# A two-layer decoder trunk on Trainium2: all 22 FFN tiles by block products, ten of them begun in the first token half

## The chip, the cores and the metric

The kernel runs on one core of one Trainium2 chip. The metric is the device time of one execution in microseconds (us): the median of several runs. The engines are named as the profile names them: PE (TensorE matmul), PEld (its weight loads), DVE (VectorE), ACT (ScalarE), POOL (GpSimd) and SP (SyncE, which issues the DMAs here).

## What is computed

Two layers, each a token mixer and a feed-forward network (FFN), on 1024 tokens of width 1024 in float32. Layer 0 mixes by gated linear attention, layer 1 by a gated delta rule. The FFN, 2816 wide, is the same in both:

```
def swiglu(h, w_gate_up, w_down):
    gate, up = jnp.split(h @ w_gate_up, 2, axis=-1)
    return (jax.nn.silu(gate) * up) @ w_down
...
        h = h + swiglu(rms_norm(h, ffn_norm_w[i]), ffn_w_gate_up[i], ffn_w_down[i])
```

## The kernel before

**Split numbers.** Every float32 operand is held as a sum hi + lo of two rounded parts. `operand` (L1114) makes them for 128x512 weights: hi by a cast on ACT (L1118), lo = src - hi on POOL (L1119). A product over k blocks of 128 rows is three matmuls per block (hi·hi, lo·hi, hi·lo, all at L201). A product over four blocks is so 12 matmuls into one 128x512 PSUM bank; over eight blocks it is 24.

**The two token halves.** The FFN works on 512 tokens at a time. The first half's normed input, called x or `head` (b11 its first four blocks, b21 the other four), is ready while the mixer still works on the second half. The mixer's last step is its output projection (`out`, 48 matmuls, w by o), and DVE adds its results into h (L316). Then comes the norm of the second half: sums of squares on ACT (L299) and DVE (L301), their total ns (L304), a reciprocal root in some ten small DVE operations, and from h and that the normed xn (L1160), which PE transposes (L1164).

**Two kinds of tiles.** A tile is 128 of the 2816 columns of gate and of up. Of the 22 tiles of a layer, 19 are computed by seven block products instead of eight: `inputsums` (L1135) makes the sums t1, t2, t3, t4 of the two halves' blocks on DVE, splits them (L1150, L1153), and `gateups` (L1198) makes the sums s1 to s4 of the four weight blocks a11, a12 (gate), a21, a22 (up) on DVE (L1208 to L1215). The seven products of 12 matmuls are a11·b11, s1·t1, s2·t2, a12·b21, s3·t3, s4·b22 and a22·t4, 84 matmuls a tile; they are added in three PSUM banks, which ACT copies out between the products (L1221 to L1230).

The other three tiles (HEAD = 3) are plain. `headparts` (L1068) computes gate and up for the first half, 24 matmuls each; after the first four blocks ACT copies what the bank holds (L1083) and SP stores it in DRAM as `part` (L1085). The end of `inputsums` (L1182 to L1196) makes the second half's gate and up from `part` (loaded at L1191) and products with t1 and b22 (`guweights`, L1121, loads the raw weights).

**Order.** In layer 0 `ffnhead` (L1064) emits the plain tiles' first halves behind the mixer. In layer 1 the order of PE is set by hand: `dense` in `gdn` is a stream of matmuls that fills the gaps of the delta rule's sequential chain, and its last two items are `headparts` and the last unit's output projection `out(UN - 1)`, which needs that unit's `post` (L1026: o scaled at L1036, transposed, gated by `gateout` at L344 to L346). Everywhere else a scheduler orders each engine's stream. The raw weights of a tile are four DMAs of 256 KB (L1130) into two buffers; the split operands have five (`wops`). `downs` is the product with w_down that follows.

## Time and profile before

| | |
|---|---|
| median of 3 runs | 3298.59 us (3297.29 to 3308.17) |
| the profiled execution | 3307.1 us, of which its span 3305.3 us |
| PE busy | 2980.4 us, 90% of the span, 14547 matmuls |
| DVE busy | 2105.8 us, 64% |
| POOL busy | 1527.4 us, 46% |
| ACT busy | 1401.0 us, 42% |
| mean granted TensorE clock | 0.956 of 2.4 GHz |

A row of a timeline gives the start, the duration, the engine, the line, what is written from what, and in brackets how long the engine sat idle before it and who released it. Busy PE is not PE at its peak: matmuls overlap, so that one is recorded as 0.39 us long and the next begins about 0.23 us after it. Durations and places in time below are those of the profiled execution.

### The profile page before, as it was taken

The page shows a single profiled execution, that of the slowest core. Times are in us where ns is not written, and L with a number is a line of the kernel's source. Part 1 is how long each engine was busy: PE and PEld are TensorE (multiplying, and loading weights), DVE is VectorE, ACT ScalarE, POOL GpSimd, SP SyncE. Part 2 cuts the span into 40 slices and gives each one's busy share as a digit, 9 for nine tenths or more (in the row PEclk, how much of TensorE's full clock was granted, in tenths as well). Part 3 has the DMA queues.
Part 4 walks back from the last instruction along what each step waited for, and adds up shares of the span by engine and source line. Part 5 has one row for each costly group of instructions (what it writes and reads, how often), then busy time and mean ns, then how long its engine had stood idle before and what let it go on. Part 6 is the DMA issues. An engine that isn't in the chain of part 4 may idle for free. (4 is left out here: it accounts for less than half of the span.)

```text
span 3305.3 us, 40855 instructions
## 1 busy us (share of the span) xinstructions
PE 2980.4 (90%) x14547; PEld 2452.3 (74%) x14547; DVE 2105.8 (64%) x4212; ACT 1401.0 (42%) x2525; POOL 1527.4 (46%) x1037
## 2 busy tenths in 40 slices
PE   6989989899998998879989897889899889999898
PEld 5877777678886777667777776777777668887776
DVE  6465665633324886778778868787788542232988
ACT  4345444434333334434445453444444434333333
POOL 4344443455555873513333333233333345554885
PEclk9999999899999999879999998999999999999999
DMA  3221222322222311312222222222232232222431
GB/s 123 77 58 58 64 64 71 104 93 77 83 83 100 133 67 41 83 31 69 70 72 69 59 59 64 64 65 67 63 77 63 84 112 78 89 83 77 143 105 58
DMA packets 364923, 256.39 MB, mean 78 GB/s; under 512 B 67848, under 2 KB 309967, under 8 KB 364719
## 3 DMA queue, kind: packets, MB, share of 16 engines
q1 hardware_dynamic: 364654, 253.77, 25.9%
q8 instruction: 114, 1.87, 0.2%
q14 instruction: 91, 0.74, 0.1%
q0 software_dynamic: 64, 0.02, 0.0%
HBM read 219.12 MB, written 34.60 MB: 77 GB/s over the span
## 5 line engine op out<-in xcount | busy, mean ns | idle before, releaser
L169 POOL TENSOR_TENSOR wlo<-raw,whi 128x1024 fp32r<-128x1024 f32 x204 | 493.3, 2420 | 772.8 <-ACT whi L168 724.5
L201 PE MATMUL pd<-xhi,whi 128*128 128x512 f32 x1072 | 450.6, 421 | 1.0 <-ACT part L1083 0.7
L201 PE MATMUL pd<-xhi,wlo 128*128 128x512 f32 x1072 | 429.6, 401 | 2.6 <-POOL wlo L169 2.6
L201 PE MATMUL pd<-xlo,whi 128*128 128x512 f32 x1072 | 427.4, 399 | 0.0
L168 ACT CAST whi<-raw 128x1024 fp32r<-128x1024 f32 x204 | 213.9, 1049 | 258.1 <-PE pd L201 133.4
L1119 POOL TENSOR_TENSOR olo<-s,ohi 128x512 fp32r<-128x512 f32 x152 | 196.0, 1291 | 206.7 <-ACT ohi L1118 206.7
L1119 POOL TENSOR_TENSOR olo<-raw,ohi 128x512 fp32r<-128x512 f32 x138 | 190.6, 1383 | 202.2 <-ACT ohi L1118 177.9
L201 PEld LDWEIGHTS pd<-xhi,wlo 128*128 128x128 f32 x1072 | 206.2, 192 | 50.9 <-POOL wlo L169 4.7
L201 PEld LDWEIGHTS pd<-xhi,whi 128*128 128x128 f32 x1072 | 207.0, 193 | 38.9 <-ACT part L1083 1.6
L201 PEld LDWEIGHTS pd<-xlo,whi 128*128 128x128 f32 x1072 | 207.3, 193 | 37.5
L1118 ACT CAST ohi<-s 128x512 fp32r<-128x512 f32 x152 | 94.3, 622 | 231.6 <-PE pd L201 175.0
L201 PE MATMUL pd<-whi,ohi 128*128 128x512 f32 x384 | 166.8, 435 | 12.3 <-ACT q L690 8.9
L886 DVE TENSOR_TENSOR xix<-xix,tmpx 128x60 f32<-128x60 f32 (+24 forms) x496 | 168.5, 340 | 13.1
L884 DVE TENSOR_TENSOR tmpx<-nbx,xix 128x60 f32<-128x60 f32 (+24 forms) x496 | 159.5, 322 | 26.3 <-DMA nbx<-d 13.5
L1118 ACT CAST ohi<-raw 128x512 fp32r<-128x512 f32 x138 | 85.1, 620 | 197.4 <-POOL olo L1119 174.3
L316 DVE TENSOR_TENSOR h<-h,pd 128x512 f32<-128x512 f32 x192 | 130.4, 682 | 55.0 <-PE pd L201 54.4
L201 PE MATMUL pd<-wlo,ohi 128*128 128x512 f32 x384 | 157.1, 409 | 2.0 <-POOL wlo L169 2.0
L201 PE MATMUL pd<-whi,olo 128*128 128x512 f32 x384 | 155.3, 404 | 0.0
L1275 POOL TENSOR_TENSOR blo<-t,bhi 128x1536 fp32r<-128x1536 f32 (+1 forms) x32 | 126.3, 3948 | 61.0 <-ACT bhi L1274 52.8
L1227 DVE TENSOR_TENSOR p<-p,pp 128x512 f32<-128x512 f32 x38 | 26.1, 688 | 196.3 <-DMA raw<-in_ffn_w_gate_up_dram 148.0
L201 PE MATMUL pd<-bhi,ahi 128*128 128x512 f32 x264 | 108.7, 412 | 36.4 <-DVE h L1285 20.1
L1275 POOL TENSOR_TENSOR blo<-rb,bhi 128x1536 fp32r<-128x1536 f32 (+1 forms) x24 | 97.8, 4074 | 42.6 <-ACT bhi L1274 42.6
(393 smaller groups left out, 8210.1 us busy)
## 6 DMA issues: line engine op xcount, KB each, us to landing
raw<-in_gdn_w_in_dram SPq DMA_DIRECT2D x96, 512.0 KB, 4.0
raw<-in_ffn_w_gate_up_dram SPq DMA_DIRECT2D x176, 256.0 KB, 3.3
raw<-in_gla_w_in_dram SPq DMA_DIRECT2D x48, 512.0 KB, 3.9
ra<-act SPq DMA_DIRECT2D x88, 256.0 KB, 5.3
rb<-in_ffn_w_down_dram SPq DMA_DIRECT2D x24, 768.0 KB, 6.5
raw<-in_gdn_w_out_dram SPq DMA_DIRECT2D x32, 512.0 KB, 3.9
act<-p SPq DMA_DIRECT2D x44, 256.0 KB, 2.0
act<-u SPq DMA_DIRECT2D x38, 256.0 KB, 2.0
```

The lines of the kernel that those rows point to most:

```text
L168: nc.scalar.copy(hi, raw)
L169: nc.gpsimd.tensor_tensor(out=lo, in0=raw, in1=hi.bitcast(F32), op=ALU.subtract)
L201: self.nc.tensor.matmul(out, lhsT, rhs, start=start, stop=stop, **kw)
L316: self.nc.vector.tensor_tensor(out=o, in0=o, in1=ps, op=ALU.add)
L884: V.tensor_tensor(out=tv, in0=nbx[:, s, s + 1:].unsqueeze(2).to_broadcast([P, m, w]), in1=xv[:, s:s + 1, 0:w].to_broadcast([P, m, w]), op= ...
L886: V.tensor_tensor(out=xv[:, s + 1:, 0:w], in0=xv[:, s + 1:, 0:w], in1=tv, op=ALU.add)
L1118: self.nc.scalar.copy(hi, src)
L1119: eng.tensor_tensor(out=lo, in0=src, in1=hi.bitcast(F32), op=ALU.subtract)
L1227: V.tensor_tensor(out=p1, in0=p1, in1=pb, op=ALU.add)
L1275: eng.tensor_tensor(out=lo, in0=src, in1=hi.bitcast(F32), op=ALU.subtract)
```

## The change

No tile is plain any more. `headparts` takes a range of tiles and computes for ten (EARLY = 10) only the first half's gate: a11·b11, which ACT copies and SP stores as `part`; then a12·b21 on top, whose Silu SP stores as `sil`. `inputsums` has no tile work left. `gateups` does each tile in two steps. `first(f)` loads part (p1) and sil, or computes them for the tiles from ten on, then s1·t1 (copied to p5) and on top of it s4·b22. `second(f)` does s2·t2, s3·t3 and a22·t4 in one bank, and adds the sums on DVE and POOL. The order is first(0), first(1), second(0), first(2), second(1) and so on, so that two tiles' raw weights are live; `wops` has four buffers instead of five. In layer 1 four of the ten early tiles stand before `out(UN - 1)` and six behind it. In matmuls per layer: before 3·(48 + 48) + 19·84 = 1884, and after 10·24 + 10·60 + 12·84 = 1848.

```diff
@@ -30,7 +30,7 @@
 C = 4
 LEVELS = (64, 32, 16, 8, 4, 2, 1)
 NT = DFF // P
-HEAD = 3
+EARLY = 10
 MASKED = -65536.0
 
 
@@ -766,8 +766,10 @@
                         yield from values(m + 1)
                         yield from late(m + 1)
                 yield ready[2]
-                yield from self.headparts(1, mx, ("v", "v", "raw"))
+                rooms = (self.tp, "v", 2), (mx, "raw", 2)
+                yield from self.headparts(1, range(4), *rooms)
                 yield from out(UN - 1)
+                yield from self.headparts(1, range(4, EARLY), *rooms)
 
             def cview(t):
                 return t.rearrange("p (c i) -> p c i", c=C)
@@ -1062,34 +1064,30 @@
 
     def ffnhead(self, l):
         self.head = self.normx(0, self.ffnw[l], self.xp, self.tp, "vch")
-        for _ in self.headparts(l):
+        for _ in self.headparts(l, range(EARLY), (self.tp, "q", 3), (self.tp, "k", 3)):
             pass
 
-    def headparts(self, l, scratch=None, tags=("q", "k", "vch")):
+    def headparts(self, l, fs, *rooms):
+
 
         nc = self.nc
-        scratch = scratch or self.tp
-        self.act = [self.dr.tile([P, T], F32, name=f"act{f}", tag=f"act{f}", bufs=2) for f in range(NT)]
-        x = self.head
-        w = self.a["ffn_w_gate_up"][l]
-        self.part = {}
-        for f in range(HEAD):
-            pss = []
-            for b in range(2):
-                ws = self.loadcols(w, [(b * DFF + f * P, P)])
-                ps = self.prepps() if b else self.dps()
-                yield from self.chanparts(ps, ws, 0, x, range(4))
-                t = self.tp.tile([P, HT], F32, name="part", tag=tags[b], bufs=2 if tags[0] == tags[1] else 3)
-                nc.scalar.copy(t, ps)
-                self.part[f, b] = d = self.dr.tile([P, HT], F32, name=f"part{f}{b}", tag=f"part{f}{b}", bufs=2)
-                nc.sync.dma_start(d, t)
-                yield 1.5
-                yield from self.chanparts(ps, ws, 0, x, range(4, 8))
-                pss.append(ps)
-            s = scratch.tile([P, HT], F32, name="s0", tag=tags[2], bufs=2)
-            nc.scalar.activation(s, pss[0], AF.Silu)
-            nc.vector.tensor_tensor(out=s, in0=s, in1=pss[1], op=ALU.mult)
-            nc.sync.dma_start(self.act[f][:, 0:HT], s)
+        room = lambda i: rooms[i][0].tile([P, HT], F32, name=("part", "sil")[i], tag=rooms[i][1], bufs=rooms[i][2])
+        if fs[0] == 0:
+            self.act = [self.dr.tile([P, T], F32, name=f"act{f}", tag=f"act{f}", bufs=2) for f in range(NT)]
+            spill = lambda n, f: self.dr.tile([P, HT], F32, name=f"{n}{f}", tag=f"{n}{f}", bufs=2)
+            self.part = [(spill("part", f), spill("sil", f)) for f in range(EARLY)]
+        for f in fs:
+            ws = self.loadcols(self.a["ffn_w_gate_up"][l], [(f * P, P)])
+            ps = self.dps()
+            yield from self.chanparts(ps, ws, 0, self.head, range(4))
+            t = room(0)
+            nc.scalar.copy(t, ps)
+            nc.sync.dma_start(self.part[f][0], t)
+            yield 1.5
+            yield from self.chanparts(ps, ws, 0, self.head, range(4, 8))
+            t = room(1)
+            nc.scalar.activation(t, ps, AF.Silu)
+            nc.sync.dma_start(self.part[f][1], t)
 
     def prod(self, ps, a, b, first=True):
 
@@ -1138,7 +1136,6 @@
         nw = self.ffnw[l]
         with ExitStack() as es:
             tp, tm = self.pool(es, "tsums", 1), self.pool(es, "ttmp", 2)
-            wr, wo = self.pool(es, "hraw", 1), self.pool(es, "hops", 3)
             new = lambda n, j: tp.tile([P, HT], F32, name=n, tag=f"{n}{j}")
 
             t1, t4 = [new("t1", j) for j in range(4)], [new("t4", j) for j in range(4)]
@@ -1179,64 +1176,66 @@
                 split("t2", j, t2[j])
                 split("t3", j, t3[j])
                 split("t4", j, t4[j])
-            for f in range(HEAD):
-
-                k = self.guweights(wr, l, f)
-                pss = []
-                for b in range(2):
-                    ps = self.seqps() if b else self.dps()
-                    self.prod(ps, self.operand(wo, k[2 * b], G), B["t1"])
-                    self.prod(ps, self.operand(wo, k[2 * b + 1], G), B["b22"], False)
-                    p = tm.tile([P, HT], F32, name="p", tag="xn")
-                    nc.sync.dma_start(p, self.part[f, b])
-                    V.tensor_tensor(out=p, in0=p, in1=ps, op=ALU.add)
-                    pss.append(p)
-                S.activation(pss[0], pss[0], AF.Silu)
-                V.tensor_tensor(out=pss[0], in0=pss[0], in1=pss[1], op=ALU.mult)
-                nc.sync.dma_start(self.act[f][:, HT:T], pss[0])
 
     def gateups(self, l, B):
         nc = self.nc
         V, S, G = nc.vector, nc.scalar, nc.gpsimd
         with ExitStack() as es:
-            wr, so, wo, tm = (self.pool(es, *x) for x in (("wraw", 2), ("wsums", 1), ("wops", 5), ("gtmp", 2)))
+            wr, so, wo, tm = (self.pool(es, *x) for x in (("wraw", 2), ("wsums", 1), ("wops", 4), ("gtmp", 2)))
             operand = lambda src: self.operand(wo, src, G)
-            for f in range(HEAD, NT):
-                a11, a12, a21, a22 = self.guweights(wr, l, f)
-                s1, s2, s3, s4 = (so.tile([P, 4, P], F32, name="s", tag=n) for n in ("s1", "s2", "s3", "s1"))
-                o11 = operand(a11)
+            half = lambda n: tm.tile([P, HT], F32, name=n, tag=n)
+            W, X = {}, {}
+
+            def first(f):
+
+                W[f] = a11, a12, a21, a22 = self.guweights(wr, l, f)
+                p1, sil = half("p1"), half("sil")
+                if f < EARLY:
+                    for t, d in zip((p1, sil), self.part[f]):
+                        nc.sync.dma_start(t, d)
+                else:
+                    pm = self.prepps()
+                    self.prod(pm, operand(a11), B["b11"])
+                    S.copy(p1, pm)
+                    self.prod(pm, operand(a12), B["b21"], False)
+                    S.activation(sil, pm, AF.Silu)
+                s1, s2, s4 = (so.tile([P, 4, P], F32, name="s", tag=n, bufs=b) for n, b in (("s1", 1), ("s2", 2), ("s1", 1)))
                 V.tensor_tensor(out=s1, in0=a21, in1=a22, op=ALU.add)
-                o1 = operand(s1)
+                pc = self.seqps()
+                self.prod(pc, operand(s1), B["t1"])
+                p5 = half("p5")
+                S.copy(p5, pc)
                 V.tensor_tensor(out=s2, in0=s1, in1=a11, op=ALU.subtract)
-                o2 = operand(s2)
-                o12 = operand(a12)
-                V.tensor_tensor(out=s3, in0=a11, in1=a21, op=ALU.subtract)
-                o3 = operand(s3)
                 V.tensor_tensor(out=s4, in0=a12, in1=s2, op=ALU.subtract)
-                o4 = operand(s4)
-                o22 = operand(a22)
-                pa, pb, pc = self.dps(), self.prepps(), self.seqps()
-                p1, p5, u2, u3 = (tm.tile([P, HT], F32, name=n, tag=n) for n in ("p1", "p5", "u2", "u3"))
-                self.prod(pa, o11, B["b11"])
-                S.copy(p1, pa)
-                self.prod(pc, o1, B["t1"])
-                S.copy(p5, pc)
-                self.prod(pa, o2, B["t2"], False)
-                S.copy(u2, pa)
-                self.prod(pb, o12, B["b21"])
-                V.tensor_tensor(out=p1, in0=p1, in1=pb, op=ALU.add)
-                S.activation(p1, p1, AF.Silu)
-                self.prod(pa, o3, B["t3"], False)
-                S.copy(u3, pa)
-                self.prod(pc, o4, B["b22"], False)
+                self.prod(pc, operand(s4), B["b22"], False)
+                X[f] = p1, sil, p5, pc, s2
+
+            def second(f):
+                a11, a12, a21, a22 = W[f]
+                p1, sil, p5, pc, s2 = X[f]
+                u2 = half("u2")
+                G.tensor_tensor(out=p5, in0=p1, in1=p5, op=ALU.add)
+                pa = self.dps()
+                self.prod(pa, operand(s2), B["t2"])
+                V.tensor_tensor(out=u2, in0=p1, in1=pa, op=ALU.add)
                 V.tensor_tensor(out=u2, in0=u2, in1=pc, op=ALU.add)
                 S.activation(u2, u2, AF.Silu)
-                G.tensor_tensor(out=p5, in0=u3, in1=p5, op=ALU.add)
-                self.prod(pa, o22, B["t4"], False)
+                s3 = so.tile([P, 4, P], F32, name="s", tag="s3")
+                V.tensor_tensor(out=s3, in0=a11, in1=a21, op=ALU.subtract)
+                self.prod(pa, operand(s3), B["t3"], False)
+                V.tensor_tensor(out=p5, in0=p5, in1=pa, op=ALU.add)
+                self.prod(pa, operand(a22), B["t4"], False)
                 V.tensor_tensor(out=u2, in0=u2, in1=p5, op=ALU.mult)
                 nc.sync.dma_start(self.act[f][:, HT:T], u2)
-                V.tensor_tensor(out=p1, in0=p1, in1=pa, op=ALU.mult)
+                V.tensor_tensor(out=p1, in0=p1, in1=pa, op=ALU.add)
+                V.tensor_tensor(out=p1, in0=p1, in1=sil, op=ALU.mult)
                 nc.sync.dma_start(self.act[f][:, 0:HT], p1)
+
+            first(0)
+            for f in range(NT):
+                if f + 1 < NT:
+                    first(f + 1)
+                second(f)
 
     def downs(self, w, act):
 
```

**PE at the end of layer 0's mixer.** The last matmuls of the output projection (w by o), then the transposes of the second half's normed xn into pp. Before:

```order
L201 MATMUL pd<-wlo,ohi 128x512
L201 MATMUL pd<-whi,olo 128x512
L1164 MATMUL pp<-cst,xn 128x128 x12
L201 MATMUL pd<-t1hi,ohi 128x512
L201 MATMUL pq<-t1hi,ohi 128x512
L201 MATMUL pd<-t1lo,ohi 128x512
L201 MATMUL pd<-t1hi,olo 128x512
L201 MATMUL pq<-t1lo,ohi 128x512
L201 MATMUL pq<-t1hi,olo 128x512
L1164 MATMUL pp<-cst,xn 128x128 x8
L201 MATMUL pd<-t1hi,ohi 128x512
```

With the change:

```order
L201 MATMUL pd<-wlo,ohi 128x512
L201 MATMUL pd<-whi,olo 128x512
L1161 MATMUL pp<-cst,xn 128x128 x32
L201 MATMUL pq<-t1hi,ohi 128x512
L201 MATMUL pq<-t1lo,ohi 128x512
```

Before, products of a plain tile with t1 stand between the transposes; now all 32 transposes stand behind the projection without a product between them, and all 240 early matmuls stand ahead of it.

**ACT at the end of layer 1's mixer.** whi and part belong to `headparts`, jk and nss to the second half's sums of squares. Before:

```order
L345 CAST ohi<-sz 128x512
L1090 ACTIVATE s_21822<-pd 128x512
L345 CAST ohi<-sz 128x512
L168 CAST whi<-raw 128x1024
L1083 COPY part<-pp 128x512
L168 CAST whi<-raw 128x1024
L299 ACTIVATE jk,nss<-h 128x512 x4
L1118 CAST ohi<-raw 128x512 x3
```

With the change:

```order
L1084 COPY part<-pd 128x512
L168 CAST whi<-raw 128x1024
L1089 ACTIVATE sil<-pd 128x512
L1084 COPY part<-pd 128x512
L1089 ACTIVATE sil<-pd 128x512
L1084 COPY part<-pd 128x512
L1089 ACTIVATE sil<-pd 128x512
L299 ACTIVATE jk,nss<-h 128x512 x4
L1166 ACTIVATE b_22184<-pp,col_rest 128x512
```

Before, the four squares stood behind the cast of the last weights; now they stand behind the Silu of the tenth early tile.

**DVE and SP in `gateups`, among the early tiles.** s<-raw at L1203 is s1 of tile f+2, made from all of a21 and a22, u at L1220 is tile f's first sum out of the bank of s2·t2. DVE before (L1208 is s1 of tile f+1, L1227 tile f's first sum):

```order
L1238 TENSOR_TENSOR p_6078<-p_6078,pd 128x512
L1213 TENSOR_TENSOR s<-raw 128x512
L1208 TENSOR_TENSOR s<-raw 128x512
L1210 TENSOR_TENSOR s<-s,raw 128x512
L1227 TENSOR_TENSOR p_6224<-p_6224,pp 128x512
L1215 TENSOR_TENSOR s<-raw,s 128x512
L1232 TENSOR_TENSOR u_6226<-u_6226,pq 128x512
```

DVE with the change:

```order
L1224 TENSOR_TENSOR s<-raw 128x512
L1203 TENSOR_TENSOR s<-raw 128x512
L1220 TENSOR_TENSOR u_5953<-p_5795,pd 128x512
L1208 TENSOR_TENSOR s<-s,raw 128x512
L1221 TENSOR_TENSOR u_5953<-u_5953,pq 128x512
L1209 TENSOR_TENSOR s<-raw,s 128x512
L1226 TENSOR_TENSOR p_5820<-p_5820,pd 128x512
L1228 TENSOR_TENSOR u_5953<-u_5953,p_5820 128x512
L1230 TENSOR_TENSOR p_5795<-p_5795,pd 128x512
L1231 TENSOR_TENSOR p_5795<-p_5795,sil 128x512
```

SP with the change; the lines of gate_up weights are the halves of the rows (2 DMAs each):

```order
L1128 DMA raw<-in_ffn_w_gate_up_dram 128x4x128 x2
L1229 DMA act_4791<-u_5953 128x512
L1232 DMA act_4791<-p_5795 128x512
L1195 DMA sil<-sil_4821 128x512
L1128 DMA raw<-in_ffn_w_gate_up_dram 128x4x128 x2
L1195 DMA p_6021<-part_4820 128x512
L1128 DMA raw<-in_ffn_w_gate_up_dram 128x4x128 x2
```

SP before, where nothing but a tile's four loads and two stores is issued:

```order
L1130 DMA raw<-in_ffn_w_gate_up_dram 128x4x128 x4
L1237 DMA act_4797<-u_6518 128x512
L1239 DMA act_4797<-p_6516 128x512
L1130 DMA raw<-in_ffn_w_gate_up_dram 128x4x128 x4
L1237 DMA act_4798<-u_6664 128x512
```

Tile f's u stands behind s1 of the tile after the next on DVE, where it was s1 of the next tile that stood ahead of a tile's first sum; and a tile's four weight loads, one run before, stand in two pairs with the loads of part and sil between them.

## Rows read from the trace of the kernel before

**Rows 1.** Window by stage: PE, PEld, DVE, ACT, POOL busy, clock, DMA share, GB/s.
```profile
605.00:672.00 67.00, 44.28 (x179) 33.03 (x178) 49.26 (x76) 27.75 (x48) 21.25 (x13) 0.85 0.39 114
```

**Rows 2.** Window in which PE never waits, in layer 0's `gateups`.
```profile
690.00:1030.00 340.00, 340.00 (x1501) 281.53 (x1500) 100.61 (x140) 133.64 (x231) 180.59 (x141) 1.00 0.24 76
```

**Rows 3.** Timeline of DVE, end of layer 0's mixer and its norm.
```profile
605.13 0.69 DVE L316 TENSOR_TENSOR h<-h,pd 128x512 f32<-128x512 f32 x1 [0.67 <-PE pd L201]
...
613.84 1.29 DVE L1160 TENSOR_TENSOR xn<-h,rs_y 128x512 f32<-128x512 f32 x2
615.82 0.75 DVE L1168 SCALAR_TENSOR_TENSOR t<-pp,col_rest,t 128x512 f32<-128x512 f32 x1 [0.69 <-PE pp L1164]
```

**Rows 4.** Timeline of DVE among the sums and splits of layer 0.
```profile
633.24 0.68 DVE L1150 TENSOR_TENSOR t3lo<-b,t3hi 128x512 fp32r<-128x512 f32 x1
633.84 0.68 DVE L1150 TENSOR_TENSOR t<-t,b 128x512 f32<-128x512 f32 x1
...
636.12 1.77 DVE L1150 TENSOR_TENSOR b<-b,t 128x512 f32<-128x512 f32 x1
```

**Rows 5.** Timeline of PE: second wait of `gateups`; start of `downs` in either layer.
```profile
672.29 0.80 PE L201 MATMUL pd<-xhi,olo 128*128 128x512 f32 x1 [4.92 <-POOL olo L1119]
...
1043.49 0.80 PE L201 MATMUL pd<-bhi,ahi 128*128 128x512 f32 x1 [8.09 <-ACT ahi L1274]
...
3056.07 0.80 PE L201 MATMUL pd<-bhi,ahi 128*128 128x512 f32 x1 [8.13 <-ACT ahi L1274]
```

**Rows 6.** Timelines of DVE and PE, end of layer 1's mixer.
```profile
2589.28 1.29 DVE L1036 TENSOR_TENSOR o<-o,rs_y 128x512 f32<-128x512 f32 x2
...
2595.61 1.41 DVE L344 SCALAR_TENSOR_TENSOR sz<-pq,col_rest,sz 128x512 f32<-128x512 f32 x2 [4.43 <-PE pq L207]
...
2598.06 0.69 DVE L346 TENSOR_TENSOR olo<-sz,ohi 128x512 fp32r<-128x512 f32 x1 [0.32 <-ACT ohi L345]
...
2592.79 0.50 PE L201 MATMUL pd<-xhi,whi 128*128 128x512 f32 x1 [0.68 <-ACT part L1083]
...
2624.81 1.97 PE L1164 MATMUL pp<-cst,xn 128*128 128x128 f32 x8 [10.40 <-DVE xn L1160]
```

**Rows 7.** Norm of layer 1 on DVE; squares on ACT (ns min/median/max).
```profile
2621.01 1.02 DVE L304 TENSOR_TENSOR ns<-nss 128x4 f32<-128x4 f32 x1
...
2624.06 1.29 DVE L1160 TENSOR_TENSOR xn<-h,rs_y 128x512 f32<-128x512 f32 x2
...
L299 ACT ACTIVATE jk<-h x32: 614/630/633, 4.4 to 2609.6; 128x512 f32<-128x512 f32 x32
...
L299 ACT ACTIVATION_READ_ACCUMULATOR jk<-h x32: 185/186/198, 4.9 to 2610.2; 128x1 f32 x32
```

**Rows 8.** Timeline, one renewal of weights: cast, lo part, DMA issue.
```profile
774.13 0.62 ACT L1118 CAST ohi<-raw 128x512 fp32r<-128x512 f32 x1 [1.60 <-POOL olo L1119]
...
774.83 1.30 POOL L1119 TENSOR_TENSOR olo<-raw,ohi 128x512 fp32r<-128x512 f32 x1 [1.42 <-ACT ohi L1118]
...
776.16 3.64 SPq L1130 DMA_DIRECT2D raw<-in_ffn_w_gate_up_dram  x4
```

**Rows 9.** Raw weights' DMAs (L1130): issue, landing; DVE's s1 (busy, mean ns).
```profile
L1130 SPq DMA_DIRECT2D raw<-in_ffn_w_gate_up_dram x176: 367/476/1758, 604.2 to 2998.6; - x176
...
DMA to landing us min/median/max: 2.8/3.3/6.6
...
L1208 DVE TENSOR_TENSOR s<-raw 128x512 f32<-128x512 f32 x17 | 11.8, 693 | 34.5 <-POOL olo L1119 34.5
```

**Rows 10.** Timeline of PE, the ends of two gaps in `downs`.
```profile
1055.39 0.50 PE L201 MATMUL pq<-bhi,alo 128*128 128x512 f32 x1 [2.68 <-DVE alo L1275]
...
1068.97 0.79 PE L201 MATMUL pq<-bhi,alo 128*128 128x512 f32 x1 [3.31 <-DVE alo L1275]
```

**Rows 11.** Windows behind these two gaps, columns as in rows 1.
```profile
1056.00:1060.00 4.00, 4.00 (x19) 3.32 (x18) 3.68 (x3) 1.39 (x3) 4.00 (x2) 1.00 0.00 0
...
1069.00:1074.00 5.00, 5.00 (x12) 3.94 (x13) 5.00 (x5) 0.00 (x0) 5.00 (x2) 0.50 0.98 326
```

## The prediction

> **What bounds the kernel now.** I read first the window by stage, then what PE waited for, then the chain of waits around it. PE is the bound nearly everywhere: in `gateups` it is busy for 340.00 of 340 us, and 1501 matmuls there make 0.2265 us each [rows 2]. What PE loses in an FFN lies ahead of `gateups`, in the second half's norm: between 605 and 672 us it works for 44.28 of 67 us, although the plain tiles give it work there [rows 1]. So two questions decide the change: what covers that norm now, and whether the new order inside `gateups` still feeds PE without a gap.
>
> **Work removed.** Per layer 1884 - 1848 = 36 matmuls, at 0.2265 us 8.2 us; 16.3 us for both layers. The sum below counts matmuls where they stand, so this is contained in it.
>
> **Layer 0, up to the first block product.** Before the output projection stand now 240 early matmuls instead of 144: 96 x 0.2265 = 21.7 us later. The projection ended at 605.1 [rows 3] and ends now at 626.8. Extra casts, copies and 256 KB stores run beside these matmuls, two tiles of which are interleaved on PE, and cost nothing as long as they do.
> Behind the projection nothing is left that covers the norm. From its end to xn is 613.84 - 605.1 = 8.7 us [rows 3]. Then DVE has 44 operations in its stream (8 xn, 12 of t1 and b22, 24 of the other sums and splits), one every 0.605 us [rows 4]: 26.6 us. Add 2 us for waits on transposes and casts (0.69 is the first of them [rows 3], the rest is an estimate from it), then s3 and s1 of tile 0 and the cast of s1, 2 x 0.65 + 0.6 = 1.9. First product: 626.8 + 8.7 + 26.6 + 2 + 1.9 = 666.0. The order decides this, not the data: t1 is ready earlier, but s1 of tile 0 stands behind the last split on DVE.
>
> **Layer 1, up to there.** With four tiles ahead of it, the last projection no longer waits for plain products. o is scaled at 2590.6; gating took 2595.61 to 2598.75, delayed by 4.43 us behind PE [rows 6]. Without that delay its operands are ready at about 2594, and 48 matmuls (10.9 us) end it at 2604.5, where it was 2614.4 (2624.81 less the 10.40 of waiting [rows 6]). Behind it six early tiles: 24 x 0.2265 + 0.7 for the copy of part, which nothing fills here (0.68 [rows 6]), 6.1 each, 36.8 in all. They do not run beside the norm, for the norm's squares on ACT stand behind the last tile's Silu. So add Silu 0.6, four squares of 0.63 with a read-out of 0.19, 3.3, and ns to xn, 2624.06 - 2621.01 = 3.05 [rows 7]: xn at 2648.3. Then the same 30.5 us on DVE as in layer 0: first product at 2678.8.
>
> **Inside `gateups`.** 1608 matmuls make 364.2 us. On top come gaps, which the kernel before does not have [rows 2].
> The main one is a loop that renews weights. Let t1's product of tile f+1 end at time 0. Only then is an operand buffer free for a22 of tile f (four buffers instead of five, two tiles alive). Cast 0.62, lo part 1.30, then SP issues the load of the second half of tile f+2's weights; in the rows of one such renewal the issue follows the cast's start by 2.03 us [rows 8]. The load is a pair; one lands 3.3 us after its issue in the median, 2.8 at best, issue itself 0.48 [rows 9], and loads of part and sil share the queue. I take 3.6 to 4.1 for the second of the pair. Then s1 on DVE 0.69 [rows 9] and its cast 0.62: t1 of tile f+2 begins at 7.1 to 7.8. PE has until then s4·b22 and s2·t2, 24 matmuls or 5.44 us; t3 stands behind t1's first matmul on PE, and tile f's u behind that s1 on DVE. Gap: 1.7 to 2.4, 1.5 with the fastest landing; I take **2.1**, seven times (tiles 3 to 9), 14.7 us.
> Start: the chains s1, cast, lo, s4, cast, lo of tiles 0 and 1 and the load of tile 2 have little PE work beside them; 4.92 us were lost at this place before [rows 5], now two tiles start, so 7 us (5 to 9). The tenth tile's change of pattern: 1.2 (0.5 to 1.3).
> The twelve late tiles have 84 matmuls, enough for the load. But s1 on DVE then runs beside a lo part on POOL. DVE took 1.77 us instead of 0.68 for such an operation in that company [rows 4]; whatever of this lands between t3 and t4 is a gap. Bounds per tile 0.15 (hand-over alone) and 1.5 (the delay of 1.09 and the hand-over twice); I take the middle, 0.75, eleven times, 8.3 us.
> The Trainium skill, SBUF — State Buffer (the section on the two sides), has VectorE and GpSimd share a port pair as an exclusive lock, so that the loser waits for the whole other instruction. By it the worst case is 1.30 + 0.69 = 1.99 us, near the 1.77 seen, so the trace agrees so far; by it each late gap could be 0.2 us longer, some 5 us in all, an estimate from that page.
> End: t3 and t4 of the last tile have no other tile's products around them, 2 us; the way into `downs` 0.4. Sum of the gaps 33.6, so `gateups` takes 397.8.
>
> **Sum.** Layer 0 ends `gateups` at 666.0 + 397.8 = 1063.8 against 1035.4 (1043.49 less 8.09 [rows 5]): +28.4. Layer 1: 2678.8 + 397.8 = 3076.6 against 3047.9 [rows 5]: +28.7. Together +57 us; what follows either stage is the same. The profiled execution took 3307.1 us and is 8.5 above the median of 3298.6; against the median the forecast is **3356 us**.
>
> **Rivals.**
> *The clock falls in the gaps.* A gap of 2.68 us left the granted clock at 1.00, one of 3.31 was followed by 0.50, the lower level of 1.2 GHz, for 12 matmuls in 5 us [rows 10, 11]; with 0.2265 us each these would have taken 2.7, so such a gap costs 2 to 3 us more. If the seven early gaps come nearer 3.3 (a landing of 5 us, where the longest was 6.6 [rows 9]), that is 14 x 2.9 = +41: about 3397. Against it: the chain gives 2.4 at most from the usual landings. The Trainium skill, TensorE: Matmul & The Clock Gate, on oscillation, tells of a kernel that waits for a DMA in every tile and falls to the low clock each time; that is this case, and no run here shows it yet.
> *The early gaps vanish.* If the second half of the weights lands within 1.6 us less than my sum, or PE's 24 matmuls come later than I read, only the start (5), the end and 0.15 a late tile remain, 8 to 9 us a layer: 666.0 + 364.2 + 8.5 - 1035.4 = +3.3, the same in layer 1, so +7: about 3305, no measurable difference.
> *Faster.* One mechanism: the covers work as the change's shape suggests, that is, PE finds early products to do while DVE works on the norm, and no wait on weights ends last. Then all gaps go (0 instead of 33.6), which gives -5 a layer, and in layer 1 the squares run beside the six tiles (-4) without stalls at the copies (-4): -18, 3281. It decides from the point where the renewed weights land 5.44 us or less after time 0 less 1.3 for s1 and its cast, that is 2.1 us after their issue. The least landing in 176 loads was 2.8 [rows 9], and the squares' place on ACT is fixed.
>
> **Chances.** Forecast with its bounds 0.70; clock 0.15; early gaps gone 0.10; faster 0.05. With the low bounds everywhere the gaps are 5 + 10.5 + 0.5 + 1.7 + 1.5 = 19.2 and the sum +28, 3327; with the high bounds 9 + 16.8 + 1.3 + 16.5 + 2.9 = 46.5, +83, 3382. The range takes in the clock's case (3397) and a few us more above, and below the low bounds the norm's uncertainty, 4 us a layer: 3318 to 3402. A difference of 0.3% (10 us) is what a measurement here tells from none. Faster 0.05; within 0.08 (nearly all of the third case); slower 0.87.
>
> **What would show it.** In layer 0's norm PE waits some 39 us with nothing but transposes. In layer 1 xn follows the last early matmul by about 7 us, and the projection ends about 10 us sooner. In `gateups` PE idles about 2 us once in each early tile, released by ACT's cast of s1, with the clock at 1.00; SP's loads of the second weight half stand right behind POOL's lo part of a22. It would be wrong if PE is busy without gaps there, if the first products begin well before 39 us behind the projection, or if the windows behind the gaps show a clock of 0.5.

## The result, and the profile of the changed kernel

The changed kernel takes **3432.69 us** (median of four runs, 3428.32 to 3442.04), the kernel before 3302.45 (four runs, 3297.29 to 3308.17). The ratio is 1.0387, 95% interval 1.0368 to 1.0406: slower by 130 us, where +57 was forecast and 3402 was the upper end of the range. The direction was right, the size was not.

The page gives the span of the profiled execution, which took 3428.32 us; its sum of PE's work is the first line of the section on busy time.

```profile
span 3426.6 us, 40832 instructions
...
PE 3011.1 (88%) x14475; PEld 2435.0 (71%) x14475; DVE 2308.1 (67%) x4324; ACT 1354.5 (40%) x2435; POOL 1536.9 (45%) x1029
```

The span is 121.3 us above that of before (3305.3). Where they are is read from PE's timeline, at the norm, the first block product and the end of `gateups` in either layer. The bracket is the idle time ahead of the row, and what ended it.

```profile
632.71 1.51 PE L1161 MATMUL pp<-cst,xn 128*128 128x128 f32 x6 [6.66 <-DVE xn L1157]
...
662.51 0.80 PE L201 MATMUL pq<-t1hi,ohi 128*128 128x512 f32 x1 [15.58 <-ACT ohi L1116]
...
1105.26 0.80 PE L201 MATMUL pd<-bhi,ahi 128*128 128x512 f32 x1 [8.34 <-ACT ahi L1273]
...
2708.29 1.97 PE L1161 MATMUL pp<-cst,xn 128*128 128x128 f32 x8 [6.48 <-DVE xn L1157]
...
2738.13 0.80 PE L201 MATMUL pq<-t1hi,ohi 128*128 128x512 f32 x1 [15.58 <-ACT ohi L1116]
...
3175.71 0.79 PE L201 MATMUL pd<-bhi,ahi 128*128 128x512 f32 x1 [8.33 <-ACT ahi L1273]
```

Layer 0's `gateups` lasts from 662.51 to 1105.26 - 8.34 = 1096.92, that is 434.4 us, and ends 61.5 later than before (1035.4, from [rows 5]). Layer 1's lasts from 2738.13 to 3175.71 - 8.33 = 3167.38, 429.3 us, and ends 119.4 later than before (3047.94), so this layer adds 57.9. The starts are close to the forecast: 662.5 for 666.0, and 2738.1 less 61.5 = 2676.6 for 2678.8. The whole excess over the forecast therefore lies between the first block product and the end of `gateups`, where 397.8 us were forecast for each layer.

What PE waited for there stands in its table of waits (us in total, times, the longest).

```profile
PE pq L201 <- ACT ohi L1116: 80.4, 19, 15.6
...
PE pd L201 <- DVE p L1226: 20.7, 24, 1.5
```

The first line holds the two waits of 15.58 behind the norm, those at the start of `gateups` and the early gaps of both layers; its releaser is the cast of s1, as forecast. The second holds the late gaps, mostly 0.65 to 0.95 each. Windows over single tiles of layer 0 show what happened to the clock (columns as in [rows 1]; the window begins about where t1 begins behind the gap).

```profile
705.80:725.90 20.10, 16.82 (x60) 12.91 (x60) 10.23 (x11) 4.26 (x8) 8.38 (x7) 0.84 0.36 106
...
745.30:764.00 18.70, 15.82 (x60) 12.17 (x60) 10.24 (x11) 4.22 (x7) 8.30 (x7) 0.91 0.38 114
...
781.10:798.60 17.50, 14.26 (x60) 11.03 (x60) 10.15 (x11) 4.13 (x8) 8.68 (x7) 1.00 0.40 120
...
859.70:1097.00 237.30, 227.21 (x964) 176.49 (x964) 120.69 (x116) 70.62 (x122) 118.95 (x89) 1.00 0.22 71
```

Sixty matmuls are 13.6 us at the rate of [rows 2]; PE has them in each of the first three windows and is busy for 16.8, 15.8 and 14.3. So the loss is not idle time alone: the matmuls themselves became longer. In the last window they do so at a clock of 1.00: 227.21 / 964 = 0.2357 us each, where before 1501 made 0.2265 [rows 2].

The renewal of weights that answers to [rows 8, 9] is the one around 717 to 726 us. Its rows on ACT, POOL, SP and DVE:

```profile
716.95 0.62 ACT L1116 CAST ohi<-raw 128x512 fp32r<-128x512 f32 x1 [0.95 <-PE pq L201]
...
717.65 1.41 POOL L1117 TENSOR_TENSOR olo<-raw,ohi 128x512 fp32r<-128x512 f32 x1 [0.28 <-ACT ohi L1116]
...
719.09 0.93 SPq L1128 DMA_DIRECT2D raw<-in_ffn_w_gate_up_dram  x2
720.12 0.45 SPq L1195 DMA_DIRECT2D p<-part  x1
720.67 0.94 SPq L1128 DMA_DIRECT2D raw<-in_ffn_w_gate_up_dram  x2
...
724.45 0.69 DVE L1203 TENSOR_TENSOR s<-raw 128x512 f32<-128x512 f32 x1 [4.84 <-DMA raw<-in_ffn_w_gate_up_dram]
...
725.25 0.62 ACT L1116 CAST ohi<-s 128x512 fp32r<-128x512 f32 x1 [7.19 <-DVE s L1203]
```

The chain is the one that the prediction wrote down, link by link: the cast of a22 when t1 of the tile before has ended, lo, the issue 2.14 after the cast's start (2.03 forecast), the landing, s1, the cast of s1. One link is longer. From the issue of the pair to DVE's start it is 5.36 us; I had taken 3.6 to 4.1. Loads of part and of the next first half are issued in between.

### The profile page after: what moved, and what is told of

It is laid out like the page before. It is cut to its first block, busy times and chain, and to the rows that moved or that the text cites. A ratio compares the mean times of both kernels' runs of the same rounds, so it can differ in the third digit from the quotient of the medians.

```text
span 3426.6 us, 40832 instructions
## 1 busy us (share of the span) xinstructions
PE 3011.1 (88%) x14475; PEld 2435.0 (71%) x14475; DVE 2308.1 (67%) x4324; ACT 1354.5 (40%) x2435; POOL 1536.9 (45%) x1029
## 5 line engine op out<-in xcount | busy, mean ns | idle before, releaser
L201 PE MATMUL pd<-xhi,whi 128*128 128x512 f32 x1184 | 495.2, 420 | 4.7 <-ACT part L1084 4.5
L201 PE MATMUL pd<-xhi,wlo 128*128 128x512 f32 x1184 | 473.8, 400 | 2.8 <-POOL wlo L169 2.8
L201 PE MATMUL pd<-xlo,whi 128*128 128x512 f32 x1184 | 471.8, 398 | 0.0
L1117 POOL TENSOR_TENSOR olo<-s,ohi 128x512 fp32r<-128x512 f32 x176 | 245.4, 1403 | 289.6 <-ACT ohi L1116 236.9
L201 PEld LDWEIGHTS pd<-xhi,wlo 128*128 128x128 f32 x1184 | 227.6, 192 | 55.9 <-POOL wlo L169 4.9
L201 PEld LDWEIGHTS pd<-xhi,whi 128*128 128x128 f32 x1184 | 228.5, 193 | 50.9 <-ACT part L1084 9.6
L201 PEld LDWEIGHTS pd<-xlo,whi 128*128 128x128 f32 x1184 | 228.2, 193 | 41.4
L1117 POOL TENSOR_TENSOR olo<-raw,ohi 128x512 fp32r<-128x512 f32 x92 | 122.1, 1327 | 118.6 <-ACT ohi L1116 118.6
L201 PE MATMUL pq<-t1hi,ohi 128*128 128x512 f32 x176 | 74.5, 423 | 80.5 <-ACT ohi L1116 80.4
L1224 DVE TENSOR_TENSOR s<-raw 128x512 f32<-128x512 f32 x44 | 75.7, 1720 | 86.3 <-POOL olo L1117 86.3
L1203 DVE TENSOR_TENSOR s<-raw 128x512 f32<-128x512 f32 x44 | 54.1, 1230 | 113.1 <-DMA raw<-in_ffn_w_gate_up_dram 109.0
```

The source lines that it names most:

```text
L201: self.nc.tensor.matmul(out, lhsT, rhs, start=start, stop=stop, **kw)
L1117: eng.tensor_tensor(out=lo, in0=src, in1=hi.bitcast(F32), op=ALU.subtract)
L1203: V.tensor_tensor(out=s1, in0=a21, in1=a22, op=ALU.add)
L1224: V.tensor_tensor(out=s3, in0=a11, in1=a21, op=ALU.subtract)
```

## Experiments

Theory A at the start: the early gaps come from the renewal of the second weight half, and its landing is late because the loads of part and sil share the queue. Rivals: the gap comes from the order of the products in `gateups` itself, whatever the landing; or the time comes from the norm, which nothing covers any more. Each result below has four runs where no other number is given, and 95% intervals against the kernel before on the same chip, whose medians there are 3304.80 to 3309.00.

**No loads of part and sil** (e1).

```diff
-                    for t, d in zip((p1, sil), self.part[f]):
-                        nc.sync.dma_start(t, d)
+                    q1 = sil = flat
```

> The ten early tiles of each layer do not load their stored part and Silu; a constant tile stands in their place, so the first half's results of these tiles are left out. Theory A (renewal loop: the gap before t1 is the wait for the second pair of weight loads, which lands 5.3 us after its issue because part and Silu are loaded beside it): the second landing falls to about 3.9 us, the early gaps from 2.4-3.5 us to 1.2-2.1, the clock stays at 1.00; per layer 8 x 1.3 + about 10 of half clock = some 20, so 40 us in all: 3380 to 3400 where the change took 3432. Theory B (the gap comes from DVE's order and its contention with POOL): gaps stay above 2 us, less than 10 us gained.

Measured: 3447.79 us, ratio 1.0422 (1.0403 to 1.0440), slower than the change by 15 us. A miss. PE's timeline in one early tile:

```profile
726.21 0.50 PE L201 MATMUL pq<-t1hi,ohi 128*128 128x512 f32 x1 [2.29 <-ACT ohi L1116]
727.56 0.50 PE L201 MATMUL pq<-t1hi,olo 128*128 128x512 f32 x1 [0.62 <-POOL olo L1117]
```

The gap before t1 did shrink; DVE's wait for weights in this tile is 3.46 us, where the change had 4.84 in the tile shown above. But PE's order was planned anew: t1's third matmul now stands ahead of t3, and PE waits a second time, for the lo part of s1. The edit changed two things at once, so it decides nothing about what the loads cost.

**Five operand buffers** (e2), paid for with a single buffer of u2.

```diff
-(("wraw", 2), ("wsums", 1), ("wops", 4), ("gtmp", 2)))
+(("wraw", 2), ("wsums", 1), ("wops", 5), ("gtmp", 2)))
-                u2 = half("u2")
+                u2 = tm.tile([P, HT], F32, name="u2", tag="u2", bufs=1)
```

> Five operand buffers instead of four (one u2 buffer instead of two pays for them). Theory A: a22's cast no longer waits for the next tile's t1 product, so the weights are asked for several us earlier; the early gaps (31 and 29 us a layer) shrink below 1 us each, the half-clock stretches (12 and 8) vanish with them: 55 to 75 us less, 3357 to 3377. Theory B: DVE's order and contention remain as they are, so the change is within 15 us of 3432.

Measured: 3464.58 us, 1.0474 (1.0453 to 1.0495). A miss. With five buffers in a ring, a22's cast waits for the slot that t4 of the tile before frees. PE's order was planned anew here too, as in e1: t1's third matmul stands ahead of t3. The gap stays and the wait for lo is added:

```profile
723.47 0.50 PE L201 MATMUL pq<-t1hi,ohi 128*128 128x512 f32 x1 [2.40 <-ACT ohi L1116]
725.89 0.80 PE L201 MATMUL pq<-t1hi,olo 128*128 128x512 f32 x1 [1.61 <-POOL olo L1117]
```

So a buffer more did not break the loop in this form of the edit; as the order moved with it, it says no more than that.

**No early tile** (e3): every tile does its seven products in `gateups`.

```diff
-EARLY = 10
+EARLY = 0
```

> No early tile at all: all 22 tiles do seven products in the new order, nothing is stored and loaded. Theory A: the late pattern costs 20.5 us a tile (row of the change's trace) for all 22, the early gaps are gone. Layer 0: norm starts 32.6 us earlier, first product 35.7 us behind it as now, 451 + 10 us of tiles: about 28 us less than the change; layer 1 loses the matmuls that filled the sequential chain, about 5 us less: 3395 to 3405, still 2.5 to 3.2% above the kernel before. Theory C (what costs is that nothing covers the norm any more, because the early tiles moved): taking the early tiles away altogether makes the norm's cover no worse, so layer 0 and 1 gain nothing but the spills: 3420 to 3435.

Measured: 3393.98 us, 1.0256 (1.0236 to 1.0275), just under the range of A. The early gaps are gone and the late ones (40 waits for p at t4, 31.2 us) remain, with the norm bare in full. Without any early tile some 85 us of the loss are still there (3393.98 - 3393.98 / 1.0256), so the stored parts are not the whole cause.

**Six early tiles behind layer 0's projection** (e4), as in layer 1.

```diff
+            for _ in self.headparts(0, range(4, EARLY), (self.tp, "q", 3), (self.tp, "k", 3)):
+                pass
-        for _ in self.headparts(l, range(EARLY), (self.tp, "q", 3), (self.tp, "k", 3)):
+        for _ in self.headparts(l, range(4), (self.tp, "q", 3), (self.tp, "k", 3)):
```

> In layer 0 six of the ten early tiles are issued behind the mixer's output projection instead of ahead of it. On ACT the squares now stand ahead of the six tiles' copies, but on PE the transposes of xn stand behind five of the six tiles. Theory A: the norm to xn (9 us) is covered and no more, the first block product comes 8 to 10 us sooner: 3420 to 3426. Theory C (any work of six tiles beside the norm covers it): 30 us sooner, 3400 to 3405.

Measured: 3417.45 us, 1.0328 (1.0309 to 1.0347): 15 us less than the change, 3 us below A's bound, but not for A's reason. PE's timeline at layer 0's first product:

```profile
660.25 0.79 PE L201 MATMUL pq<-t1hi,ohi 128*128 128x512 f32 x1 [17.32 <-ACT ohi L1118]
```

It comes 2.3 us sooner than in the change, where 8 to 10 were expected. The profiled execution is 10.2 us shorter than the change's, and 7.9 of these lie in layer 0's `gateups` (426.5 us for 434.4), most of it in fewer matmuls at the low clock. So the near hit is luck: this place for the early tiles covers little of the norm.

**PE's order as the program has it** (e5): the planner's freedom on PE taken away, nothing else.

```diff
+            es.enter_context(self.tc.manual_schedule(engines={mybir.EngineType.PE}))
```

> The change with PE's stream in gateups in the order in which the program is written: t1 and s4*b22 of tile f+1, then t2, t3, t4 of tile f; nothing else is edited. Theory A (the weights are renewed late, and the scheduler's order, with t1 of tile f+2 ahead of t3 and t4 of tile f, exposes that): 48 matmuls or 10.9 us lie now between t1 of f+1 and t1 of f+2 instead of 24, so the gap of 2.4 to 3.5 us before t1 goes; instead t2, t3 and t4 in one bank wait for DVE's sums, 1.3 and 0.9 us a tile as at the end of the change's gateups (rows of its trace), for all 22 tiles: some 53 us a layer where there are 70, the clock at 1.00: 3390 to 3405. Theory B (two tiles' weights alive with two buffers: the weights come late in any order): the gap before t1 stays above 2 us in the early tiles and the bank's waits are added: 3430 or more.

Measured: 3679.26 us, 1.1131 (1.1114 to 1.1148). A's range is missed by 275 us. B's bound (3430 or more) holds, but not its reason: no gap stands before t1. PE's timeline in one early tile, at t3:

```profile
752.19 0.50 PE L201 MATMUL pd<-t3hi,ohi 128*128 128x512 f32 x1 [3.65 <-DVE u L1221]
```

DVE's timeline ahead of it, the last row being the u that releases t3's bank:

```profile
749.75 1.07 DVE L1204 TENSOR_TENSOR s<-raw 128x512 f32<-128x512 f32 x1 [7.67 <-DMA raw<-in_ffn_w_gate_up_dram]
750.85 0.69 DVE L1209 TENSOR_TENSOR s<-s,raw 128x512 f32<-128x512 f32 x1
751.46 0.68 DVE L1221 TENSOR_TENSOR u<-p,pd 128x512 f32<-128x512 f32 x1
```

t3 needs the bank that u reads. u stands on DVE behind s1 of the tile after next, which waits 7.67 us for weights. The wait for weights reaches PE through DVE's queue even when t1 is not next on PE. This formed the theory that held: what matters is the order on PE and on DVE together, that is, what stands in either queue behind the operation that waits for the weights.

**An order written out by hand** (e6): one tile at a time on PE as t2(f), b22(f), t3(f), t1(f+1) or b11(f+1), t4(f), where t1(f) stands for the product s1·t1 of tile f, and so on. a22's operand is made before the next tile's s1, and DVE's operations stand in the same order. The split into first and second is undone; products, buffers, stored parts and the norm are those of the change. Condensed:

```diff
-            for f in range(NT):
-                if f + 1 < NT:
-                    first(f + 1)
-                second(f)
+            t1(0)
+            for f in range(NT):
+                if late(f): b21(f)
+                if f + 1 < NT: load(f + 1)
+                t2(f); b22(f); t3(f)
+                if late(f + 1): b11(f + 1); t4(f); t1(f + 1)
+                elif f + 1 < NT: t1(f + 1); t4(f)
+                else: t4(f)
```

> The same products, sums and early tiles as in the change, but PE's order in gateups by hand: t2 and s4*b22 of tile f, t3, then t1 (or a11*b11) of tile f+1, then t4 of tile f, so that another bank's product stands between any two of one bank, and a tile's weights are let go before its last product. Theory A: no gap is left in either pattern but the start (5 us) and the tail; gateups takes about 364 + 8 instead of 434 and 429: 115 to 125 us less than the change, 3308 to 3318, level with the kernel before although the norm is as bare as in the change. Theory B (contention of DVE and POOL, or DMA traffic of part and Silu, holds PE up): gaps of 1 us or more a tile stay, 3350 or more.

Measured: 3307.79 us (ten runs, 3299.94 to 3313.19), 1.0004 (0.9992 to 1.0016). A hit, 125 us below the change. Windows over early and over late tiles of layer 0:

```profile
672.00:790.00 118.00, 117.92 (x521) 97.32 (x520) 79.23 (x88) 36.75 (x61) 73.69 (x53) 1.00 0.50 154
800.00:1025.00 225.00, 225.00 (x994) 186.30 (x993) 110.66 (x115) 75.00 (x128) 127.22 (x94) 1.00 0.23 73
```

PE has no gap, the clock is 1.00, and 994 matmuls make 0.2264 us each, as before. PE's timeline at the first product of either layer:

```profile
662.59 0.79 PE L201 MATMUL pq<-t1hi,ohi 128*128 128x512 f32 x1 [15.57 <-ACT ohi L1116]
...
2677.90 0.79 PE L201 MATMUL pq<-t1hi,ohi 128*128 128x512 f32 x1 [15.57 <-ACT ohi L1116]
```

Both stand behind the same wait as in the change, so the norm is as bare as there. `gateups` takes 368.8 and 369.3 us, 125.6 less over both layers. The DMA engines carry more here (154 GB/s) than in the change's early tiles (106 to 120 in the windows above), with the same loads of part and sil. So neither these loads nor the norm made the 125 us; the order in `gateups` did. It also fits that this kernel is no faster than before: 16.3 us of matmuls are saved, and the cover of the norm is lost.

**The two halves of that order** (e7): the change's order in the early tiles, by hand (g1, g2 and g4 are the products with t1, t2 and b22, p3 the one with t3), and e6's order in the late ones. Condensed:

```diff
-            for f in range(NT):
+            for f in range(EARLY - 2):
+                raws(f + 2); s1t1(f + 2)
+                go(X[f + 2]["g1"], 1)
+                uadd(f); p3(f)
+                go(X[f + 2]["g1"], 4)
+                t4(f); rest(f + 2)
+                go(X[f + 2]["g1"], 7)
...
+            for f in range(EARLY, NT):
```

> PE's order written by hand: in the early tiles exactly the change's (t1 of tile f+2: 1, t3 of f, t1: 4, t4 of f, t1: 7, t2 of f+1: 5, s4*b22 of f+2, t2: 7), in the late tiles that of the hand-ordered run before. DVE and SP keep the change's order in the early tiles. It is the base of the next run, and says what the early tiles alone cost: their gaps (31 and 29 us a layer), half-clock stretches (12 and 8) and spaced first matmuls (7) stay, the late tiles' 18 to 20 us a layer go: 3385 to 3400.

Measured: 3391.97 us, 1.0260 (1.0238 to 1.0282). A hit. The early tiles' order alone costs 3391.97 - 3307.79 = 84 us, the rest of the change's order 3432.69 - 3391.97 = 41.

**The same, without the loads of part and sil** (e8), with PE's order held fixed this time.

```diff
-                    for t, d in zip((x["p1"], x["sil"]), self.part[f]):
-                        nc.sync.dma_start(t, d)
+                    x["q1"], x["sil"] = flat, flat
```

> As the run before, with PE's order held, but the early tiles do not load their stored part and Silu; a constant tile stands in their place, so these tiles' first half is left out. Theory A (these loads delay the second pair of weights from 3.5-3.9 us to 5 us, and that pushes the gap from 2 us to 3 and lets the clock fall): the landing is back at 3.5 to 4, gaps 1.3 us shorter, no half clock: 35 to 45 us less, 3345 to 3360. Theory B (the gap has its length from DVE's and ACT's chains, and the clock falls for other reasons): less than 12 us gained.

Measured: 3422.32 us, 1.0362 (1.0344 to 1.0380): 30 us slower than e7. Both expectations missed. POOL, SP and PE in one tile:

```profile
757.27 1.41 POOL L1127 TENSOR_TENSOR olo<-raw,ohi 128x512 fp32r<-128x512 f32 x1 [0.28 <-ACT ohi L1126]
...
759.26 2.04 SPq L1138 DMA_DIRECT2D raw<-in_ffn_w_gate_up_dram  x4
...
766.28 0.79 PE L201 MATMUL pq<-t1hi,ohi 128*128 128x512 f32 x1 [3.95 <-ACT ohi L1126]
```

Without the two small loads SP's queue closes up: the four weight loads go out as one burst, a first-half load of a later tile stands ahead of the second-half pair that s1 waits for, and the pair's last load is issued some 1.6 us after lo has ended (760.25 against 758.68; in the change 0.5). The gap is 3.95 us. Theory A falls as the cause of the loss: with these loads gone the pair's last load lands sooner in e1 (3.45 us after its issue in the tile shown, 4.84 in the change's) and hardly sooner here (4.54), and neither kernel gained. What stands ahead of the pair on SP counts too, not the two loads alone.

**A third buffer for the second weight half** (e10), on e7's order, again with one buffer of u2.

```diff
-            raw = pool.tile([P, 4, 2, P], F32, name="raw", tag=f"raw{kh}")
+            raw = pool.tile([P, 4, 2, P], F32, name="raw", tag=f"raw{kh}", bufs=2 + kh)
```

> The replica of the change's PE order, with one thing added: three buffers instead of two for the second half of the raw weights (one u2 buffer instead of two pays for them), so that this half of tile f+2 is asked for a tile earlier, while DMA traffic, products and PE's order stay. Theory A (what costs is that this half is asked for only after a22's lo part, and DVE queues the first sum of tile f behind it): the gaps before t1 in the early tiles vanish, and with them the half clock: 3392 less 75 to 95, 3297 to 3317. Theory B (traffic of part, Silu and weights in one burst, or DVE beside POOL, sets the gap): gaps of 1.5 us and more stay, 3350 to 3390.

Measured: 3346.83 us, 1.0125 (1.0103 to 1.0146), between the two expectations. The load no longer waits for a22's lo part, and the gap before t1 is gone. PE's timeline has another one, at t3:

```profile
755.30 0.50 PE L201 MATMUL pd<-t3hi,ohi 128*128 128x512 f32 x1 [1.36 <-DVE u L1311]
```

DVE's timeline shows what the u there stood behind:

```profile
753.96 0.69 DVE L1293 TENSOR_TENSOR s<-raw,s 128x512 f32<-128x512 f32 x1 [3.34 <-POOL olo L1127]
754.57 0.68 DVE L1311 TENSOR_TENSOR u<-p,pd 128x512 f32<-128x512 f32 x1
```

A line of PE's table of waits, and a window over early tiles of layer 0:

```profile
PE pd L201 <- DVE u L1311: 23.9, 18, 1.7
...
677.00:800.00 123.00, 113.47 (x481) 88.18 (x480) 75.50 (x79) 33.72 (x56) 60.62 (x48) 1.00 0.45 137
```

On DVE, u stands behind s4, which waits 3.34 us for POOL's lo part; in e7 u stood ahead of s4, so DVE's order moved with the edit. The clock holds 1.00 over these gaps in this profile, which is of the fastest of the four runs (3340.32). The renewal is thereby shown to make the gap before t1: break it and 45 of the 84 us go, as a net figure that has the new waits in it. Of the 39 that are left, much is the head of the next queue (18 waits of this kind, 23.9 us).

**A version that covers the norm** (e9): e6's order, four tiles ahead of the projection, and the other six early tiles in `inputsums`, their products by hand between the norm's transposes.

```diff
-        for _ in self.headparts(l, range(EARLY), (self.tp, "q", 3), (self.tp, "k", 3)):
+        for _ in self.headparts(l, range(FIRST), (self.tp, "q", 3), (self.tp, "k", 3)):
...
+            e = early()
+            for _ in range(LEAD):
+                next(e, None)
...
             for j in range(4):
+                next(e, None)
```

> The hand-ordered gateups, and six of the ten early tiles of each layer computed inside the second half's norm: PE's order there by hand, three early products, then the transposes of each pair of blocks with an early product between, then the rest; squares stand ahead of the early casts on ACT. Theory A (an uncovered norm is what is left of the change's loss): the first block product comes some 45 us behind the projection with 32.6 us of early matmuls in that time, 20 to 28 us less a layer: 3250 to 3270, faster than both. Theory C (twelve more lo parts on POOL slow DVE's 44 sums and splits down so far that the cover is eaten up): 3290 to 3310.

Measured: **3272.29 us** (3268.46 to 3276.39), 0.9901 (0.9886 to 0.9916): 2 us above the expected range, and faster than both kernels. PE's timeline at the first product of either layer:

```profile
646.93 0.79 PE L203 MATMUL pq<-t1hi,ohi 128*128 128x512 f32 x1 [8.85 <-ACT ohi L1117]
...
2643.86 0.80 PE L203 MATMUL pq<-t1hi,ohi 128*128 128x512 f32 x1 [8.67 <-ACT ohi L1117]
```

A window beside layer 0's norm, columns as in [rows 1]:

```profile
600.00:640.00 40.00, 35.68 (x167) 28.40 (x165) 31.92 (x44) 27.14 (x49) 15.14 (x10) 0.99 0.39 126
```

PE works 35.68 of 40 us beside the norm, and the first products come 15.7 (layer 0) and 34.0 us (layer 1, both layers together) sooner than in e6; that is the 35.5 us between the two.

**Twelve early tiles** (e11): the same with EARLY = 12, for the 8.85 us that are left.

```diff
-EARLY = 10
+EARLY = 12
```

> The version with the covered norm and twelve early tiles instead of ten, eight of them beside the norm: 48 more matmuls (10.9 us) move from behind the norm into it. 8.9 us of waiting were left there in layer 0 and 8.7 in layer 1. Theory A: that wait goes, 6 to 9 us less a layer: 3254 to 3262 where ten tiles took 3272. Theory C (DVE's chain grows with the additional lo parts on POOL and stays behind PE): no gain, 3268 to 3276.

Measured: 3268.61 us, 0.9887 (0.9863 to 0.9911). A's range is missed, and C's (no gain, 3268 to 3276) holds: not to be told from e9. The wait before the first product falls from 8.85 to 5.69 us in layer 0 and from 8.67 to 5.46 in layer 1. But layer 0's first product comes 11.5 us later (658.38), about as much as `gateups`, with 48 matmuls fewer, is shorter (10.8).

## Why the prediction was right in part

**Right: the direction and its two places.** No cover for the norm and gaps in `gateups` were the two terms forecast, and both are there. The first products were foretold within 3.5 and 2.2 us. The 39 us of bare norm in layer 0 are 36.4 (from the last sum's start at 626.09 to 662.51).

**Right, nearly: the idle time in `gateups`.** The rows of waits, term by term, in layer 0 and layer 1 against the forecast: start 6.0 and 5.8 (7 forecast); the seven early gaps 20.6 and 18.8 (14.7); the change of pattern 1.7 and 1.7 (1.2); the eleven late gaps 8.6 and 10.2 (8.3); end 2.2 and 2.2 (2, and 0.4 for a hand-over). Sum 39.1 and 38.7 for 33.6. The late gaps were mostly 0.65 to 0.95 long (two of them 1.34 and 1.48) for 0.75. The early gap was under-sized, 2.9 and 2.7 us for 2.1, mostly by the one link named above: the landing. The forecast's own sum is loose there: its links as listed (2.03, 3.6 to 4.1, 0.69 and 0.62) give 6.94 to 7.44 us, not 7.1 to 7.8. So is a sum in layer 1, where 2594 and 10.9 make 2604.9, not 2604.5; neither changes the outcome.

**Wrong: "1608 matmuls make 364.2 us."** This is the step that failed. `gateups` less its idle time is 434.4 - 39.1 = 395.3 us in layer 0 and 429.3 - 38.7 = 390.6 in layer 1, so the same 1608 matmuls cost 31 and 26 us more. The rate of 0.2265 was read in a stretch where PE never waits [rows 2] and carried into one where it waits 26 times. Two things lengthen them. Rows of PE behind three early gaps, start and length in us:

```profile
725.92 0.80 PE L201 MATMUL pq<-t1hi,ohi 128*128 128x512 f32 x1 [3.21 <-ACT ohi L1116]
726.52 0.63 PE L201 MATMUL pd<-t3hi,ohi 128*128 128x512 f32 x1
726.94 0.63 PE L201 MATMUL pd<-t3lo,ohi 128*128 128x512 f32 x1
...
745.35 0.67 PE L201 MATMUL pq<-t1hi,ohi 128*128 128x512 f32 x1 [2.51 <-ACT ohi L1116]
745.82 0.63 PE L201 MATMUL pd<-t3hi,ohi 128*128 128x512 f32 x1
...
781.19 0.50 PE L201 MATMUL pq<-t1hi,ohi 128*128 128x512 f32 x1 [2.94 <-ACT ohi L1116]
781.53 0.40 PE L201 MATMUL pd<-t3hi,ohi 128*128 128x512 f32 x1
```

First, the clock. Behind the gaps of 3.21 and 2.51 us the matmuls start 0.427 us apart, the lower level of 1.2 GHz; 61 such spacings in layer 0 and 38 in layer 1 cost (0.427 - 0.2265) each, 12.2 and 7.6 us; spacings of 0.59 to 0.77 us just behind such gaps add 3.5 and 3.6. That is 26.9 us. The forecast priced this at nothing, as a rival with 41 us behind the fourteen early gaps and a chance of 0.15. Behind these gaps it is 15.8 us, more than a third of that; the rest stands behind the norm and at the start of `gateups`. A clock of 0.5 behind the gaps, which the prediction named as a sign that it was wrong, stands in the windows of the last section. Of the seven windows behind the early gaps in layer 0, five have a mean clock of 0.84 to 0.91 and two of 1.00; of layer 1's seven, three have 0.85 to 0.92 and four 0.99 or 1.00. The Trainium skill, TensorE: Matmul & The Clock Gate, on oscillation, describes a kernel that waits for a DMA in each tile and falls to the low clock each time; this trace agrees with it in eight gaps of fourteen.

Second, at full clock, the matmuls around every wait and every late operand. The first matmul behind a gap is followed 0.335 us later instead of 0.2265 (781.19 to 781.53), its own start costs 0.16 more than the idle time shows, and where the bank changes the same happens with no idle time on record:

```profile
784.98 0.39 PE L201 MATMUL pq<-t1lo,ohi 128*128 128x512 f32 x1
785.24 0.50 PE L201 MATMUL pd<-t4hi,ohi 128*128 128x512 f32 x1
785.58 0.40 PE L201 MATMUL pd<-t4lo,ohi 128*128 128x512 f32 x1
```

Spacings of over 0.245 at such hand-overs, some 100 in each layer, add 7.4 and 7.0 us to what the gaps add; with those behind the gaps, the gaps' own starts and spacings of 0.23 us it is 15.3 and 15.2 us. In e6, where operands are ready ahead of time, two spacings of over 0.245 at full clock are left in layer 0. That the late operands cause it is my reading; what is shown is that it goes with the order.

**Check of the sum.** Over both layers `gateups` took 863.7 us for 795.6 forecast, +68.1: idle time +10.6, clock +26.9, lengthened matmuls +30.5. Less the 5.7 by which the starts came early, this is 62.4, and +57 (with its roundings) becomes the 119.4 that the trace shows. The same parts can be read from PE's timeline of the other kernels: the two layers' `gateups` together, above 1608 matmuls at 0.2265 in each, in us. Low clock is what spacings of 0.38 us and more have above 0.2265, and lengthened is what remains.

| | idle | low clock | lengthened |
|---|---|---|---|
| the change | 77.8 | 26.9 | 30.5 |
| e1 | 79.8 | 39.8 | 34.8 |
| e7 | 59.6 | 24.0 | 13.5 |
| e8 | 72.5 | 41.9 | 12.6 |
| e10 | 30.5 | 4.9 | 13.2 |
| e6 | 2.2 | 6.1 | 1.3 |

So e1 lost against the change mostly by the clock, and e8 against e7 by the clock and the idle time.

**The rivals.** *The early gaps vanish* and *Faster* are refuted by the rows above. *Faster* named as its mechanism that PE finds early products while DVE works on the norm; e9 shows that this was a fair idea for the wrong kernel: in the change no early product stands beside layer 0's norm, and with them there it is worth 35.5 us. In layer 1 the six tiles behind the projection stood ahead of the norm, as forecast.

**Still open.** Of the 84 us of the early order e10 explains 45 by the renewal. The other 39 are idle time and lengthened matmuls (30.5 and 13.2 for 2.2 and 1.3 in e6); u's place on DVE, hand-overs and the start were not tried apart. The change's 41 us outside the early order are about half late gaps and half lengthened matmuls (e7 has 18 and 17 us less of them); what in the late order makes them was not tried either.

## What to carry to other kernels

A rate per matmul holds only for a stretch that waits as little as the one it was read in: when a change adds a wait to every tile, price the idle time, then the clock behind it, then the matmuls around each hand-over, which here cost 26.9 and 30.5 us beside 77.8 of idle time. Ask of each operation that waits for a transfer what stands behind it in its engine's queue and in SP's: a further buffer moved the wait to the next entry (e10; in e2 it stayed, with PE's order changed), while an order that puts nothing urgent behind the waiting one removed it (e6). Work that is meant to cover a serial stage must stand beside it in PE's order, or it covers nothing (e6 against e9).
